# RMSNorm with ReLU on one core: from two DMA queues and strided 2 MB chunks to one queue in fixed order and contiguous 4 MB chunks

## The chip, the cores and the metric

The kernel runs on 1 core of one Trainium2 chip. The metric is the time of one execution on the device in microseconds (us); a lower number is better. In the views ACT is ScalarE, DVE is VectorE, POOL is GpSimd and SP is SyncE, which here only issues transfers; a DMA engine is one of the 16 that move the data. A profile describes one execution and gives its span, from the first to the last instruction; the measured time of the same execution is 1.8 to 2.1 us longer than its span.

A ratio is the mean time of one kernel's fast runs over the mean time of the other kernel's fast runs in the same rounds on the same chip, so it is not quite the ratio of the medians that are quoted beside it.

## The reference

```python
# x: [16, 1024, 512] float32 (32 MiB), gamma: [512] ones, eps = 1e-5
rms = np.sqrt(np.mean(x ** 2, axis=-1, keepdims=True) + eps)
x_norm = x / rms * gamma
return np.maximum(x_norm, 0).astype(np.float32)
```

There are 16,384 rows of 512 numbers. 33.55 MB have to be read and 33.55 MB written.

## The kernel before

Each of the 128 partitions owns 128 consecutive rows and takes them 8 at a time (16 KB per partition, 2 MB per transfer, neighbouring partitions 256 KB apart in DRAM). Loads are issued from SP (a hardware queue), stores from POOL (the software queue). The store converts a bf16 tile to f32 on its way. Gamma is spread over all partitions by a broadcast load of 256 KB that stands in front of the first load of x.

```python
xv = x2.rearrange("(p r) d -> p r d", p=P)
ov = out2.rearrange("(p r) d -> p r d", p=P)
K = 8
...
gamma_bcast = bass.AP(tensor=gamma.tensor, offset=gamma.offset,
                      ap=[[0, P], gamma.ap[0]])
nc.sync.dma_start(out=gamma_sbuf, in_=gamma_bcast)
...
for i in range(nchunks):
    s = i * K
    x_tile = pool.tile([P, K, d], F32)            # pool has 4 buffers
    nc.sync.dma_start(out=x_tile, in_=xv[:, s:s + K, :])
    ...
    nc.vector.tensor_mul(out=xg, in0=x_tile, in1=gammaK)
    for j in range(K):
        nc.scalar.activation(out=sq_scratch, in_=x_tile[:, j, :], func=Square,
                             accum_out=ss[:, j:j + 1])
    nc.scalar.activation(out=rms, in_=ss, func=Sqrt, bias=eps_sbuf, scale=inv_d)
    nc.vector.reciprocal(out=rstd, in_=rms)
    for j in range(K):
        nc.vector.tensor_scalar(out=o_tile[:, j, :], in0=xg[:, j, :],
            scalar1=rstd[:, j:j + 1], scalar2=0.0, op0=mult, op1=max)
    nc.gpsimd.dma_start(out=ov[:, s:s + K, :], in_=o_tile)
```

Of the kernel before, what the change touches and what calls it, by code (L numbers as in the profile page):

```python
# [1 line left out]

# [4 lines left out]


@with_exitstack
def kernel(  # L10
    ctx: ExitStack,
    tc: tile.TileContext,
    x: bass.AP,
    gamma: bass.AP,
    eps: bass.AP,
    out: bass.AP,
):
    nc = tc.nc
    P = nc.NUM_PARTITIONS

    x2 = x.flatten_outer_dims()
    out2 = out.flatten_outer_dims()
    n, d = x2.shape
    assert n % P == 0
    rows_per_part = n // P
    inv_d = 1.0 / d

    xv = x2.rearrange("(p r) d -> p r d", p=P)
    ov = out2.rearrange("(p r) d -> p r d", p=P)

    K = 8
    nchunks = rows_per_part // K
    assert rows_per_part % K == 0

    BF = mybir.dt.bfloat16
    F32 = mybir.dt.float32

    singles = ctx.enter_context(tc.tile_pool(name="singles", bufs=1))
    pool = ctx.enter_context(tc.tile_pool(name="pool", bufs=4))
    small = ctx.enter_context(tc.tile_pool(name="small", bufs=4))  # L40

    gamma_sbuf = singles.tile([P, d], F32)
    gamma_bcast = bass.AP(
        tensor=gamma.tensor,
        offset=gamma.offset,
        ap=[[0, P], gamma.ap[0]],
    )
    nc.sync.dma_start(out=gamma_sbuf, in_=gamma_bcast)  # L48

    eps_sbuf = singles.tile([P, 1], F32)  # L50
    nc.vector.memset(eps_sbuf, eps)  # L51

    sq_scratch = singles.tile([P, d], F32)

    gammaK = bass.AP(tensor=gamma_sbuf.tensor, offset=gamma_sbuf[:].offset,
                     ap=[gamma_sbuf[:].ap[0], [0, K], gamma_sbuf[:].ap[1]])

    for i in range(nchunks):
        s = i * K

        x_tile = pool.tile([P, K, d], F32)
        nc.sync.dma_start(out=x_tile, in_=xv[:, s:s + K, :])

        rstd = small.tile([P, K], F32)
        rms = small.tile([P, K], F32)
        ss = small.tile([P, K], F32)
        xg = pool.tile([P, K, d], F32)
        o_tile = pool.tile([P, K, d], BF)

        nc.vector.tensor_mul(out=xg, in0=x_tile, in1=gammaK)  # L70

        for j in range(K):
            ssj = ss[:, j:j + 1]
            nc.scalar.activation(out=sq_scratch, in_=x_tile[:, j, :],  # L74
                                 func=mybir.ActivationFunctionType.Square,
                                 accum_out=ssj)
        nc.scalar.activation(out=rms, in_=ss,  # L77
                             func=mybir.ActivationFunctionType.Sqrt,
                             bias=eps_sbuf, scale=inv_d)
        nc.vector.reciprocal(out=rstd, in_=rms)  # L80

        for j in range(K):
            rj = rstd[:, j:j + 1]
            nc.vector.tensor_scalar(  # L84
                out=o_tile[:, j, :], in0=xg[:, j, :],
                scalar1=rj, scalar2=0.0,
                op0=mybir.AluOpType.mult, op1=mybir.AluOpType.max,
            )

        nc.gpsimd.dma_start(out=ov[:, s:s + K, :], in_=o_tile)  # L90


# [1 line left out]
_INS = ['x', 'gamma', 'eps']  # L94
_OUTS = [((16, 1024, 512), 'float32')]
#: Inputs that are plain numbers.
_NUMBERS = {'eps': 9.999999747378752e-06}


# [26 lines left out]
```

## Time and profile before

| | before |
|---|---|
| time, median (range) | 165.87 us (165.78 to 166.01) |
| span of the profile | 164.0 us |
| DMA | 67.4 MB, 411 GB/s over the span |
| DVE busy, ACT busy | 75%, 61% |

These lines are from the page of the kernel before. The digits cut the span into 40 slices and give the busy share in tenths; the GB/s line has one number per slice; a queue's line gives its packets, megabytes and share of the time of 16 engines.

```profile
span 164.0 us, 565 instructions
...
DVE 122.8 (75%) x161; ACT 99.4 (61%) x274; POOL 8.9 (5%) x20
...
DMA  5999999999999999999999999999999999998994
GB/s 87 401 420 444 440 412 432 434 432 412 436 436 412 440 434 424 424 432 436 412 436 436 414 432 436 412 440 432 428 424 432 432 416 436 440 432 348 416 420 192
...
q1 hardware_dynamic: 2448, 33.82, 57.4%
q0 software_dynamic: 2304, 33.56, 49.4%
q14 instruction: 3, 0.02, 0.0%
```

The DMA engines are the busy ones and no compute engine is near 100%. The weak slices are the first (87 GB/s), one near the end (348) and the last.

The windows view of the kernel before gives, for each stretch: its length, busy time of DVE, ACT and POOL, the clock, the DMA share and GB/s.

```profile
core 0: us, DVE busy (x) ACT busy (x) POOL busy (x), PEclk, DMA share, GB/s
0.00:4.00 4.00, 0.06 (x1) 1.28 (x1) 0.20 (x4) 1.00 0.56 88
144.00:148.00 4.00, 4.00 (x3) 3.84 (x11) 0.00 (x0) 1.00 1.05 426
148.00:152.00 4.00, 3.96 (x11) 1.41 (x5) 0.53 (x1) 1.00 0.80 324
152.00:156.00 4.00, 2.15 (x6) 0.00 (x0) 0.53 (x1) 1.00 1.11 455
```

In the first 4 us little moves. From 148 to 152 us the DMA engines lose a quarter of their rate.

### The profile page before, as it was taken

The numbers are of one execution on the slowest core, as the hardware profiler recorded it, in microseconds if no ns is written. First come the engines' busy times: TensorE is split into PE (matmuls) and PEld (weight loads), VectorE is DVE, ScalarE is ACT, GpSimd is POOL, SyncE is SP. The second block draws the span as 40 slices with busy tenths as digits, with TensorE's granted clock in tenths as the row PEclk, the third lists the DMA queues.
The fourth block names the chain that finished last, engine by engine and source line by source line (L and its number), as shares of the span: only waits on it lengthen the run. The fifth ranks groups of instructions, "written<-read, shape, count | busy, mean of one in ns | idle before, by whom it ended". The sixth has DMA issues, their size and how long they took to land.

```text
span 164.0 us, 565 instructions
## 1 busy us (share of the span) xinstructions
DVE 122.8 (75%) x161; ACT 99.4 (61%) x274; POOL 8.9 (5%) x20
## 2 busy tenths in 40 slices
DVE  0029979999999999969498694968949498099600
ACT  3039999999993937739195682928649194094000
POOL 0000010011010101010100001010010101001100
DMA  5999999999999999999999999999999999998994
GB/s 87 401 420 444 440 412 432 434 432 412 436 436 412 440 434 424 424 432 436 412 436 436 414 432 436 412 440 432 428 424 432 432 416 436 440 432 348 416 420 192
DMA packets 4755, 67.40 MB, mean 411 GB/s; under 512 B 528, under 2 KB 528, under 8 KB 656
## 3 DMA queue, kind: packets, MB, share of 16 engines
q1 hardware_dynamic: 2448, 33.82, 57.4%
q0 software_dynamic: 2304, 33.56, 49.4%
q14 instruction: 3, 0.02, 0.0%
HBM read 33.82 MB, written 33.55 MB: 411 GB/s over the span
## 4 chain that ended last, share of the span: by engine, by line
issue 49%; DVE 27%; ACT 8%; DMA 6%; POOL 3%; POOLq 0%; SPq 0%
DVE xg L70 15%; DVE o_tile L84 11%; ACT sq_scratch L74 7%; DMA x_tile<-in_x_dram 6%; POOL out_dram L90 3%; ACT L77 1%; DVE rstd L80 1%; ACT rms L77 0%; POOLq L121 0%; SPq L48 0%; POOLq L90 0%
## 5 line engine op out<-in xcount | busy, mean ns | idle before, releaser
L74 ACT ACTIVATE sq_scratch<-x_tile 128x512 f32<-128x512 f32 x128 | 80.6, 630 | 48.8 <-DMA x_tile<-in_x_dram 45.3
L70 DVE TENSOR_TENSOR xg<-x_tile,gamma_sbuf 128x4096 f32<-128x4096 f32 x16 | 70.5, 4406 | 29.3 <-DMA x_tile<-in_x_dram 29.3
L84 DVE TENSOR_SCALAR o_tile<-xg,rstd 128x512 bf16<-128x512 f32 x128 | 52.1, 480 | 0.1
L74 ACT ACTIVATION_READ_ACCUMULATOR sq_scratch<-x_tile 128x1 f32 x128 | 23.9, 187 | 0.0
L90 POOL DMA_DIRECT2D out_dram<-o_tile x16 | 8.7, 541 | 145.9 <-DVE rstd L80 119.4
L77 ACT ACTIVATE rms<-ss,eps_sbuf 128x8 f32<-128x8 f32 x16 | 4.8, 301 | 0.5
L80 DVE RECIPROCAL rstd<-rms 128x8 f32<-128x8 f32 x16 | 3.1, 196 | 1.2 <-ACT rms L77 1.2
L74 ACT ACT_TABLE_LOAD x1 | 1.3, 1283 | 0.7 <-PEq L107 0.7
L77 ACT ACT_TABLE_LOAD x1 | 1.3, 1283 | 0.0
L51 DVE MEMSET eps_sbuf<- 128x1 f32 x1 | 0.1, 59 | 0.8 <-PEq L107 0.8
L107 POOL MEMSET const-float32-0.0<- 128x1 f32 x1 | 0.1, 99 | 0.2 <-issue 0.2
L107 POOL MEMSET const-bfloat16-1.0<- 128x1 bf16 x1 | 0.1, 102 | 0.0
L107 POOL MEMSET const-float32-1.0<- 128x1 f32 x1 | 0.1, 99 | 0.0
L107 POOL MEMSET const-uint8-127<- 128x1 uint8 x1 | 0.1, 99 | 0.0
## 6 DMA issues: line engine op xcount, KB each, us to landing
x_tile<-in_x_dram SPq DMA_DIRECT2D x16, 2048.0 KB, 26.4
out_dram<-o_tile POOLq DMA_DIRECT2D x16, 2048.0 KB, 21.3
gamma_sbuf<-in_gamma_dram SPq DMA_DIRECT2D x1, 256.0 KB, 5.4
```

What stands on the lines that cost most here:

```text
L51: nc.vector.memset(eps_sbuf, eps)
L70: nc.vector.tensor_mul(out=xg, in0=x_tile, in1=gammaK)
L74: nc.scalar.activation(out=sq_scratch, in_=x_tile[:, j, :], func=mybir.ActivationFunctionType.Square, accum_out=ssj)
L77: nc.scalar.activation(out=rms, in_=ss, func=mybir.ActivationFunctionType.Sqrt, bias=eps_sbuf, scale=inv_d)
L80: nc.vector.reciprocal(out=rstd, in_=rms)
L84: nc.vector.tensor_scalar(out=o_tile[:, j, :], in0=xg[:, j, :], scalar1=rj, scalar2=0.0, op0=mybir.AluOpType.mult, op1=mybir.AluOpType.max,)
L90: nc.gpsimd.dma_start(out=ov[:, s:s + K, :], in_=o_tile)
L107: nc = _bacc.Bacc("TRN2", target_bir_lowering=False, num_devices=1)
```

## The change

The intent is one stream of transfers that never pauses: all loads and stores in one hardware queue (SP) in an order fixed in the program, each transfer 4 MB and contiguous in DRAM (32 KB per partition), six slots of 4 MB that are loaded, computed in place in f32 and stored. Gamma becomes four loads of one 2 KB row on the ACT queue and a shuffle on DVE, and no longer stands in front of x. The squares that ACT throws away go to PSUM. The diff, cut to its core:

```diff
-    xv = x2.rearrange("(p r) d -> p r d", p=P)
-    ov = out2.rearrange("(p r) d -> p r d", p=P)
-    K = 8
+    xv = x2.rearrange("(c p k) d -> c p k d", p=P, k=16)
+    ov = out2.rearrange("(c p k) d -> c p k d", p=P, k=16)
+    K = 16
+    G = 8
+    nslots = 6
 ...
-    nc.sync.dma_start(out=gamma_sbuf, in_=gamma_bcast)
+    for q in range(0, P, 32):
+        nc.scalar.dma_start(out=gseed[q:q + 1, :], in_=gamma[None, :])
 ...
+    def load(i):
+        nc.sync.dma_start(out=slot[i % nslots], in_=xv[i])
+    def store(i):
+        nc.sync.dma_start(out=ov[i], in_=slot[i % nslots])
+    def compute(i):
+        xt = slot[i % nslots]
+        for g in range(ngroups):                  # two groups of 8 rows
+            a, b = g * G, (g + 1) * G
+            for j in range(a, b):
+                nc.scalar.activation(out=junk, in_=xt[:, j, :], func=ACTF.Square,
+                                     accum_out=ss[i][:, j:j + 1])
+            nc.scalar.activation(out=rms[i][:, a:b], in_=ss[i][:, a:b],
+                                 func=ACTF.Sqrt, bias=eps_sb, scale=inv_d)
+            nc.vector.tensor_mul(out=xt[:, a:b, :], in0=xt[:, a:b, :], in1=gammaG())
+            nc.vector.reciprocal(out=rstd[i][:, a:b], in_=rms[i][:, a:b])
+            for j in range(a, b):
+                nc.vector.tensor_scalar(out=xt[:, j, :], in0=xt[:, j, :],
+                    scalar1=rstd[i][:, j:j + 1], scalar2=0.0, op0=ALU.mult, op1=ALU.max)
 ...
-        nc.gpsimd.dma_start(out=ov[:, s:s + K, :], in_=o_tile)
+    for i in range(min(nslots, nchunks)):
+        load(i)
+    nc.vector.stream_shuffle(gamma_sb, gseed, [0] * 32)
+    for i in range(min(nslots, nchunks)):
+        compute(i)
+    nxt = nslots
     for i in range(nchunks):
+        store(i)
+        if i >= 1 and nxt < nchunks:
+            load(nxt)
+            compute(nxt)
+            nxt += 1
```

The order in the queue is load 0 to 5, store 0, store 1, load 6, store 2, load 7, store 3 to 7.

## The prediction

> **What bounds it now: DMA.** The page gives 67.4 MB in a 164.0 us span, 411 GB/s, the DMA engines at 9 tenths in 37 of 40 slices; DVE is 75% busy, ACT 61%. The landings in the trace sharpen this. Before the first store, 2 MB loads land every 4.90 us (428 GB/s); once a 2 MB load and a 2 MB store alternate, a pair takes 9.79 us (428 GB/s again). So one queue loading and two queues mixing run at one rate: 612 ns per 16 KB packet and engine. The Trainium skill, "DMA: Bandwidth & Descriptors", section "Specifications", gives a 435 GB/s fabric ceiling; this trace sits 2% below it. At 428, 67.1 MB need 156.7 us (estimate). Only about 7 us of the span are not that.
>
> **Where those 7 us are (packets of the trace).** The first packet starts at 1.75 us, but belongs to the gamma broadcast: 128 packets of 2 KB, many of 200 to 800 ns, so the first x packets start at 3.2 to 5.7 us, engine by engine. Near 148 to 152 us the queue runs thin (324 GB/s in the windows view; stores wait for DVE): about 1 us. The last store packet ends at 162.15, lands at 162.5; the span ends 1.5 us later.
>
> **What the change does.**
> - Gamma's broadcast becomes four 2 KB rows on the ACT queue plus a shuffle. x packets should start near 1.8 us: 1.5 to 3 us gained, all on the critical path. Largest term.
> - The dip near 150 us goes, as the last loads are queued early and stores follow back to back: about 1 us.
> - One queue instead of two, 4 MB contiguous chunks, 32 KB per partition: no change of rate, since 428 holds in both phases now; at most 1 us if packets grow beyond 16 KB.
> - Compute stays hidden. DVE per 8 rows: 4.29 + 3.17 + 0.11 = 7.57 us (chain of waits), 15.1 per chunk, 121 in all; now f32 to f32 in place, and I expect that to cost the same. New wait: the multiply overwrites x, so it waits for ACT's eight squares (8 x 0.755 = 6.0 us), exposed in the first group only. The first chunk lands near 12 us, DVE starts at 18 and ends near 140; the queue reaches the last store near 149 (1.8 + 15 x 9.8). Slack 9 us. The first store is ready at 34 us, the six loads occupy the queue until 60, and each reload waits for a store that finishes with another transfer queued. No bubble.
>
> **Sum.** 1.9 start + 156.7 data + 0.3 gamma remnants and skew + 0.4 landing + 1.5 end = 160.8, minus 0.5 for larger packets = 160.3 us span. The measured time is 1.9 us above the span now (165.87 against 163.97), so about 162.0 us: 2.3% faster, close to the 2% line. Range 159.9 to 164.2. Faster 0.63, same 0.32, slower 0.05.
>
> **What would show it.** Right: first x packets near 1.8 us; GB/s near 428 in every slice but the first and last; 9.8 us between 4 MB landings; last store issued before its turn. Wrong: DVE ending after 149 us; gaps in the GB/s line at load-to-store turns; first chunk landing after 13 us.
>
> **What would make it wrong.** In-place f32 scaling at half rate (0.6 us a row adds 25 us to DVE and makes it the bound, about 172 us); hardware-queue stores slower than the software-queue ones, never seen in this trace; a contiguous layout changing the 612 ns packet either way.

## The result, and the profile after

| | before | after |
|---|---|---|
| time, median (range), 4 runs each | 165.82 us (165.5 to 166.01) | 164.24 us (163.98 to 164.49) |
| ratio, 95% interval | 1 | 0.9904 (0.9888 to 0.9921) |
| span of the profile | 164.0 us | 162.0 us |

The kernel is 1% faster, which counts as the same at the 2% line. The prediction said 2.3% and 159.9 to 164.2 us; the measured time lies just outside the range. A later repeat of the changed kernel (run e14) gave 164.26 us and a ratio of 0.9914.

The same lines of the page, of the changed kernel:

```profile
span 162.0 us, 554 instructions
...
DVE 124.6 (77%) x164; ACT 98.5 (61%) x274; POOL 0.2 (0%) x4
...
DMA  6999899999999999998999999999999999999990
GB/s 227 421 405 502 388 413 493 390 421 477 396 421 471 396 388 388 461 445 388 463 437 404 453 445 404 453 437 396 461 429 445 429 421 445 429 421 445 437 413 16
...
q1 hardware_dynamic: 2304, 67.11, 96.9%
q14 instruction: 3, 0.02, 0.0%
q10 hardware_dynamic: 8, 0.01, 0.0%
```

The start is better (227 GB/s instead of 87). The ups and downs of the GB/s line are packets of 32 KB falling into one slice or the next. The end is odd: one slice at 413, then one at 16. The windows view of the changed kernel shows it closer:

```profile
0.00:4.00 4.00, 0.49 (x2) 0.79 (x1) 0.20 (x4) 1.00 0.69 229
144.00:148.00 4.00, 0.00 (x0) 0.00 (x0) 0.00 (x0) 1.00 0.99 426
148.00:152.00 4.00, 0.00 (x0) 0.00 (x0) 0.00 (x0) 1.00 0.97 418
152.00:156.00 4.00, 0.00 (x0) 0.00 (x0) 0.00 (x0) 1.00 1.02 442
156.00:160.00 4.00, 0.00 (x0) 0.00 (x0) 0.00 (x0) 1.00 0.51 221
160.00:162.00 2.00, 0.00 (x0) 0.00 (x0) 0.00 (x0) 1.00 0.00 0
```

The dip at 148 us is gone as predicted, and DVE is done before. But the half of the DMA time that is used from 156 to 160 us is nearly all before 158 us (410 GB/s from 156 to 158 us, 33 from 158 to 160 us), while the last landing comes only at 160.97 us, with nothing left to issue. The waits of SP, the engine that issues the transfers, in the changed kernel (who waited for what: total us, times, longest us) show that it was done early:

```profile
SPq L62 <- DVE slot L81: 94.5, 7, 20.7
SPq L59 <- DMA out_dram<-slot: 30.5, 2, 22.1
SPq L133 <- DMA out_dram<-slot: 17.6, 1, 17.6
```

The last line is SP at the end of the program, waiting 17.6 us for stores that it has long issued. So neither compute nor issue holds up the end; the DMA engines do. What they do can be read from the landings: each of the 16 engines reports separately when its sixteenth of a transfer has landed. The Trainium skill says so in "DMA: Bandwidth & Descriptors", section "Why a DMA increments its semaphore by 16 and not by 1" (the engines "finish independently"), and the traces here show the 16 separate times. This table is worked out from those times, for the last transfer of each profile. "Lag" is the last engine minus the ninth of 16.

```
profile                    9th engine   15th    last    lag   fetches in the run
before                        162.29   162.36  162.52   0.23   3
after                         158.86   159.42  160.97   2.11   3
e1  no gamma loads            158.98   160.99  161.22   2.24   3
e2  copy only                 158.67   158.86  159.03   0.35   0
e3  more instructions         158.85   160.82  162.44   3.59   9
e4  before + gamma rows       159.98   160.29  160.52   0.54   3
e5  copy + instructions       158.82   159.47  164.00   5.18   6
e6  strided rows              159.90   161.87  161.87   1.98   3
e7  16 KB runs                159.24   160.62  162.04   2.80   3
e8  two hardware queues       177.03   177.10  177.13   0.09   3
e9  markers                   158.86   161.36  161.40   2.54   3
e10 copy, alternating         159.09   159.22  159.65   0.56   0
e11 stores on POOL queue      158.69   159.14  160.20   1.50   3
e12 few instructions          158.94   159.70  160.26   1.31   0
e13 few, no gamma loads       158.74   159.13  159.99   1.26   0
e14 changed kernel again      158.81   160.54  161.27   2.46   3
```

In the changed kernel a middle engine has everything landed at 158.9 us, one engine needs until 161.0, and the program ends with that one. The lag does not come at once. From the same landings of the changed kernel it is 0.50 us at the landing of load 2 (32 us), 0.78 at load 4 (52 us), 1.05 at load 5 (63 us), 1.58 at load 6 (93 us), 1.34 at store 2 (102 us), 2.10 at load 7 (113 us) and 2.11 at the end. The instruction fetches of this profile (8 KB packets of queue 14) start at 31.5, 50.9 and 79.8 us.

### The profile page after: what moved, and what is told of

The parts are those of the page before. It is cut to its first block, busy times and chain, and to the rows that moved or that the text cites. A ratio compares the mean times of both kernels' runs of the same rounds, so it can differ in the third digit from the quotient of the medians.

```text
span 162.0 us, 554 instructions
## 1 busy us (share of the span) xinstructions
DVE 124.6 (77%) x164; ACT 98.5 (61%) x274; POOL 0.2 (0%) x4
## 4 chain that ended last, share of the span: by engine, by line
DVE 74%; DMA 8%; ACT 3%; issue 2%; DVEq 0%
DVE slot L78 43%; DVE slot L81 30%; DMA slot<-in_x_dram 8%; ACT junk L74 3%; DVE rstd L79 1%; DVEq L133 0%
## 5 line engine op out<-in xcount | busy, mean ns | idle before, releaser
L74 ACT ACTIVATE junk<-slot 128x512 f32<-128x512 f32 x128 | 76.8, 600 | 23.0 <-DMA slot<-in_x_dram 19.5
L78 DVE TENSOR_TENSOR slot<-slot,gamma_sb 128x4096 f32<-128x4096 f32 x16 | 70.7, 4418 | 4.2 <-ACT junk L74 4.2
L81 DVE TENSOR_SCALAR slot<-slot,rstd 128x512 f32<-128x512 f32 x128 | 52.1, 481 | 0.6
L74 ACT ACTIVATION_READ_ACCUMULATOR junk<-slot 128x1 f32 x128 | 23.8, 186 | 0.0
L76 ACT ACTIVATE rms<-ss,eps_sb 128x8 f32<-128x8 f32 x16 | 4.8, 301 | 0.5
L86 DVE MEMSET gseed<- 128x512 f32 x1 | 0.5, 485 | 0.9 <-PEq L119 0.9
L93 DVE STREAM_SHUFFLE gamma_sb<-gseed 128x512 f32<-128x512 f32 x1 | 0.7, 721 | 0.0
```

The lines of the kernel that those rows point to most:

```text
L74: nc.scalar.activation(out=junk, in_=xt[:, j, :], func=ACTF.Square, accum_out=ss[i][:, j:j + 1])
L76: nc.scalar.activation(out=rms[i][:, a:b], in_=ss[i][:, a:b], func=ACTF.Sqrt, bias=eps_sb, scale=inv_d)
L78: nc.vector.tensor_mul(out=xt[:, a:b, :], in0=xt[:, a:b, :], in1=gammaG())
L81: nc.vector.tensor_scalar(out=xt[:, j, :], in0=xt[:, j, :], scalar1=rstd[i][:, j:j + 1], scalar2=0.0, op0=ALU.mult, op1=ALU.max)
L86: nc.vector.memset(gseed, 0.0)
L93: nc.vector.stream_shuffle(gamma_sb, gseed, [0] * 32)
```

## The experiments

The theory at this point: a transfer is cut into 16 fixed shares, so the program ends with the slowest DMA engine, and some engines carry small extra transfers (fetches, gamma rows). The rivals: the late engine is late for a reason in the data transfers themselves, or in the traffic of ACT and DVE to the tiles, or compute is on the path after all.

| run | time, median (range) us | ratio to before (95%) | result |
|---|---|---|---|
| e1 no gamma loads | 164.07 (163.82 to 164.35) | 0.9895 (0.9878 to 0.9911) | right |
| e2 copy only | 161.67 (161.52 to 161.79) | 0.9751 (0.9737 to 0.9764) | wrong |
| e3 more instructions | 165.66 (165.48 to 165.87) | 0.9992 (0.9980 to 1.0005) | right |
| e4 before + gamma rows | 163.68 (163.62 to 163.76) | 0.9872 (0.9859 to 0.9886) | right |
| e5 copy + instructions | 166.08 (165.74 to 166.62) | 1.0024 (1.0007 to 1.0041) | wrong |
| e6 strided rows | 165.14 (164.72 to 165.56) | 0.9965 (0.9948 to 0.9981) | right |
| e7 16 KB runs | 164.28 (163.55 to 165.03) | 0.9912 (0.9886 to 0.9938) | right |
| e8 two hardware queues | 180.11 (179.78 to 182.42) | 1.0885 (1.0843 to 1.0926) | right |
| e9 markers | 164.28 (2 runs) | 0.9912 (0.9890 to 0.9933) | right |
| e10 copy, alternating | 163.63 (162.25 to 164.63) | 0.9870 (0.9832 to 0.9907) | wrong |
| e11 stores on POOL queue | 162.98 (162.66 to 163.98) | 0.9840 (0.9815 to 0.9864) | right |
| e12 few instructions | 162.85 (162.36 to 163.21) | 0.9818 (0.9802 to 0.9834) | wrong |
| e13 few, no gamma loads | 162.33 (161.92 to 162.93) | 0.9796 (0.9778 to 0.9814) | wrong |
| e14 changed kernel again | 164.26 (163.95 to 164.90) | 0.9914 (0.9897 to 0.9931) | right |

Most of these differences are under the 2% line (only e2 counts as faster, e8 as slower, e13 is unclear), so below they are read from the ratios to the kernel before, whose runs stood in the same rounds, and from the landings. The landings of a run are those of its one profile.

### e1: without the gamma loads

```diff
-    nc.vector.memset(gseed, 0.0)
+    nc.vector.memset(gseed, 1.0)
-    for q in range(0, P, 32):
-        nc.scalar.dma_start(out=gseed[q:q + 1, :], in_=gamma[None, :])
```

> The changed kernel with the four gamma loads taken out (gamma set to ones by a memset; it is ones in this input, so the result stays right). Theory S (one DMA engine ends 1.6 to 2.1 us after the others because it alone carries small extra transfers: four gamma rows of about 84 ns each and instruction fetches of about 0.32 us each): the spread of the last landing (last against middle engine, now 2.1 us) shrinks by about 0.35 us and the time by about 0.3 us, to about 163.9. Rival P (the late engine is late for a reason in the data transfers themselves): no change of the spread, under 0.1 us in time.

The ratio moved by 0.1% (0.9895 against 0.9904), within noise, and the lag stayed (2.24 us). So the gamma rows are not what makes the last engine late. In this profile two engines are late, at 160.99 and 161.22 us. This part of my theory fell.

### e2: copy only

```diff
     def compute(i):
-        (all of the computing)
+        pass
```

The gamma loads and the shuffle were taken out as well; the output is wrong.

> Wrong on purpose: the changed kernel's sixteen transfers in their order, with all computing and gamma taken out, so almost no instructions are fetched. Theory S: the last engine's lag at the end falls from 2.1 us to under 0.5 us; the start at 1.75 us, the long first packets (0.65 us) and the long packets at the first load-to-store turn (about 0.65 us near 58 us) stay; span about 160.0, time about 162.1. Rival P: the lag of about 2 us stays and the time is 163.5 or more. If the compute engines were on the path (rival C), the time would fall by over 3 us, to below 161.

161.67 us, 2.5% faster than before, and the lag is 0.35 us. The middle engine is hardly earlier than in the changed kernel (158.67 against 158.86): the gain lies in the late engine. Compute is not on the path. The queue lines of its page show what else left with the compute: there is no line for instruction fetches.

```profile
DMA packets 2304, 67.11 MB, mean 420 GB/s; under 512 B 256, under 2 KB 256, under 8 KB 256
...
q1 hardware_dynamic: 2304, 67.11, 98.1%
```

### e3: more instructions

```diff
+    pad = singles.tile([P, 1], F32, name="pad")
+    for _ in range(768):
+        nc.gpsimd.memset(pad, 0.0)
```

> The changed kernel with 768 tiny memsets (128x1, about 0.1 us each) on the idle POOL engine, which touch nothing else. Theory S: they need about six more 8 KB instruction fetches (64 bytes an instruction is an estimate from 8 KB fetches and the counts), each 0.32 us on some DMA engine; if they share the late engine, its lag grows by about 1 to 2 us and the time with it, to 165.2 to 166.2. Rivals P and C: within 0.2 us of the changed kernel.

The ratio went from 0.9904 to 0.9992 (about 1.5 us), the fetches from 3 to 9 and the lag to 3.59 us, with the middle engine unmoved at 158.85. POOL work that touches none of the kernel's data made it slower, as the theory said. e3 still had all the compute in it, so e5 asks the same of a kernel with none.

### e4: the kernel before, with only gamma changed

```diff
-    nc.sync.dma_start(out=gamma_sbuf, in_=gamma_bcast)
+    gseed = singles.tile([P, d], F32)
+    nc.vector.memset(gseed, 0.0)
+    for q in range(0, P, 32):
+        nc.scalar.dma_start(out=gseed[q:q + 1, :], in_=gamma[None, :])
+    nc.vector.stream_shuffle(gamma_sbuf, gseed, [0] * 32)
```

> The kernel before, with only its gamma broadcast replaced by the four row loads and the shuffle. My prediction's largest term says: x packets start near 1.8 us, not 3.2 to 5.7, and the time falls by 1.5 to 3 us, to 163 to 164.4. If the early start is given back later (to the wait of stores for DVE near 140 to 152 us, or to the late engine), less than 1 us is left.

163.68 us: 2.1 us gained, in the middle of what I expected, from this part alone. The windows view of e4, same columns as before:

```profile
0.00:4.00 4.00, 0.49 (x2) 1.13 (x1) 0.20 (x4) 1.00 0.61 209
144.00:148.00 4.00, 4.00 (x9) 3.05 (x9) 0.00 (x0) 1.00 1.07 434
```

209 GB/s in the first 4 us instead of 88. So this line of the change is worth more than the whole change (ratio 0.9872 against 0.9904 and 0.9914), and all the rest of it, the one queue, the order, the 4 MB chunks, costs 0.3% to 0.4% on balance. The landings say where: against e4 the middle engine of the changed kernel is done 1.1 us earlier (158.86 against 159.98), the last one 0.45 us later (160.97 against 160.52).

### e5: copy only, with instructions on POOL

```diff
     (e2, and)
+    pad = singles.tile([P, 1], F32, name="pad")
+    for _ in range(768):
+        nc.gpsimd.memset(pad, 0.0)
```

> Wrong on purpose: the copy-only kernel (161.67 us; all 16 engines end within 0.4 us of the middle one) with the 768 tiny memsets on POOL added, nothing else. Theory F (instruction fetches of 8 KB delay the DMA engine that carries them, each by 0.3 us and more): about six fetches appear in the trace at 10 to 145 us and some engines end late; if they share few engines as in the run with more instructions, the time rises by 0.6 to 1.6 us, to 162.3 to 163.3. Rival T (the late engines come from the traffic of ACT and DVE to the tiles, which copy-only also took out): no late engine, 161.7 again.

The direction was right and the size was far off: 166.08 us, 4.4 us more than e2, not 0.6 to 1.6. The trace of e5 has six fetches, at 11.0, 31.0, 52.3, 72.0, 92.0 and 112.3 us. Up to the first one POOL had started 74 instructions, then 202, 338, 464, 592, 721: one fetch about every 128 instructions. One single engine is late, at 164.00 us, with the other 15 done by 159.47; at every landing since the second fetch, too, only one is late. The page of e5:

```profile
GB/s 246 390 455 437 406 469 398 463 421 406 485 382 471 413 382 382 445 439 398 493 382 437 447 406 477 398 429 455 406 469 398 453 429 421 461 398 461 429 143 16
...
q1 hardware_dynamic: 2304, 67.11, 95.3%
q14 instruction: 6, 0.05, 0.1%
```

0.05 MB of fetches, 0.1% of the DMA time, and the kernel is 2.7% slower than e2, because all six went through one engine (read from the landings; the packets carry no engine number). The last slice (16 GB/s) is that engine alone, and so is the end of the one before (143). The second fetch moved its lag from 0.54 to 1.19 us between two neighbouring landings, the third from 1.20 to 2.04: 0.65 and 0.84 us, though the fetch's own packet is recorded with 0.31 us. Part of the rest is in the trace: the data packet that follows each fetch is longer too, by 0.09 to 0.35 us. Not all of the 5.18 us belongs to fetches: from 2.04 to 3.13 us the lag grew between the landings at 53.6 and 65.0 us, with no fetch between them, where the first store follows the loads. The memsets came with the fetches and no run parts the two, but POOL ran them at an even pace, and the lag sits on one engine and grows in steps. There is no ACT and no DVE work in this run, so the rival that blamed their traffic falls as an explanation of this lag.

### e6: old row layout, all else changed

```diff
-    xv = x2.rearrange("(c p k) d -> c p k d", p=P, k=16)
+    xv = x2.rearrange("(p c k) d -> c p k d", p=P, k=16)     # and ov the same
```

> The changed kernel with the old row layout (each partition owns 128 consecutive rows, so a 4 MB chunk is 128 runs of 32 KB, 256 KB apart, not one contiguous block). If contiguity in DRAM does nothing, as I predicted: within 0.3 us of the changed kernel (164.1). If it is what makes the steady packet short (1213 ns for 32 KB), packets get longer by 1% or more and the time rises by 1.5 us or more.

Neither. The median packet stayed at 1213 ns, so contiguity does nothing for the steady rate. Yet the time is 165.14 us, ratio 0.9965, 0.5% to 0.6% worse than the changed kernel. The middle engine ends 1.0 us later (159.90). The chains of packets in the trace show longer packets where the queue turns from loads to stores: near 58 to 60 us the engines lose 0.9 to 1.4 us on two packets (0.3 to 1.2 in the changed kernel), and near 90 us most lose another 0.4 to 0.8 us (0 to 0.3 in the changed kernel, but for its late engine). So contiguous chunks are worth about 0.9 us here, at the turns. Why, no run shows.

### e7: runs of 16 KB inside the 4 MB transfers

```diff
-    xv = x2.rearrange("(c p k) d -> c p k d", p=P, k=16)
+    xv = x2.rearrange("(c h p k) d -> c p h k d", h=2, p=P, k=8)   # ov and the tile side alike
```

> The changed kernel, same 4 MB transfers and order, but each partition's 32 KB come as two runs of 16 KB from the two halves of the chunk, so packets are 16 KB. If the packet size gave the 1% (1213 ns for 32 KB against 2 x 611.5): steady spacing of landings 9.78 instead of 9.68 us, time up by about 1.3 us, to 165.4, less what a smaller first packet saves (about 0.3). If the packet size does nothing: 164.1.

The packets became 16 KB (median 611 ns). Loads landed every 9.79 us instead of 9.72 and stores every 9.70 instead of 9.68. The middle engine ended 0.4 us later. The time (164.28 us, and a wide spread) shows no difference, so the packet size is worth less than the 1.3 us I gave it; the verdict on the time is open.

### e8: loads from ACT, stores from SP

```diff
-        nc.sync.dma_start(out=slot[i % nslots], in_=xv[i])
+        nc.scalar.dma_start(out=slot[i % nslots], in_=xv[i])     # and gamma's rows from SP
```

> The changed kernel with loads issued from ACT and stores from SP (and gamma's four rows from SP), so that stores may share the engines with loads from 34 us on. If the long packets near 58 us (0.6 to 0.7 us on every engine) are the price of all engines turning from loads to stores at once in one queue, they go, and the time falls by 0.4 to 0.8 us, to about 163.4; the late engines stay. If the one-queue order costs nothing: within 0.2 us of 164.1, or slower if mixed packets of 32 KB are less regular.

180.11 us, and it does not answer the question. ACT also computes the squares and works in program order, so the last reloads stood behind the squares of the chunks before: in the timeline of e8 the issue of load 6 comes only at 97.1 us.

```profile
97.13 0.33 ACTq L59 DMA_DIRECT2D slot<-in_x_dram  x1
```

The next two lines, from the page of e8, show the queues running dry.

```profile
DMA  6989989989999999999999999999938999200595
GB/s 235 472 369 456 463 375 456 458 368 375 449 441 406 449 441 412 441 456 406 427 463 405 427 463 412 419 471 412 412 103 375 405 419 471 118 0 0 235 471 235
```

### e9: markers

```diff
+    sets = {1: (3, 6, 9, 12, 15), 4: (1, 4, 7, 10, 13), 5: (2, 5, 8, 11, 14)}
     for i in range(min(nslots, nchunks)):
         load(i)
+        for k in sets.get(i, ()):
+            mk = singles.tile([16, 64], F32, name=f"mk{k}")
+            nc.sync.dma_start(out=mk[0:k, :], in_=x2[0:k, 0:64])
```

> A kernel for looking, not for its time: the changed kernel without the gamma loads, with 15 small marker loads of k rows (k = 1 to 15, 256 bytes each) between the big loads of the one queue. If a load of k rows goes to the k lowest-numbered engines, the number of markers in a chain of packets tells which engine it is. Theory F expects the same two late engines at the end as in the run without gamma loads (1.7 to 2.1 us behind the middle), each carrying a fetch near 32 and 80 us or near 51 us; the markers say which numbers they have. No claim about the numbers.

Again two late engines (161.36 and 161.40 us, the other 14 by 159.25), and the fetches at 33.3, 51.2 and 80.5 us. The Trainium skill, "DMA: Bandwidth & Descriptors", section "Why a DMA increments its semaphore by 16 and not by 1", says that a DMA from a hardware queue that runs on k engines takes the k lowest-numbered. The trace shows k landings of data for a marker of k rows. Read together, the landings name the late ones. Of the two landings of the marker with 2 rows one is late (63.98 against 62.38 us); the marker with 1 row was not late (52.01 us); among the 4 landings of the marker with 4 rows two are late (52.87 and 52.91 against 52.07 us). That makes them engine 1 and engine 2 or 3, and not engine 0, where the single gamma rows would go. This fits e1, in which taking the gamma rows away changed nothing. It rests on the skill's rule, which no run here tests by itself.

### e10: copy only, alternating

```diff
     (e2, and the order of the queue)
+    load(0)
+    for i in range(nchunks):
+        if i + 1 < nchunks:
+            load(i + 1)
+        store(i)
```

> Wrong on purpose: copy only, with loads and stores alternating from the start (load 0, load 1, store 0, load 2, store 1, ...), so about fifteen turns between reading and writing instead of six. If each turn costs what the first one did (0.5 to 0.7 us on every engine), the time rises from 161.7 by 3 us or more. If only the first store pays, or a turn costs 0.1 us: 161.4 to 162.5, and the long packets stand at the first store, near 22 us.

The times scatter from 162.25 to 164.63 us, so they don't decide. The one profile (of the fastest run) shows one packet of nearly every engine longer by 0.6 to 1.0 us at 20.8 to 21.0 us, when the first store follows, and almost nothing longer than 0.15 us at the turns after it. In that profile the first store costs once, wherever it stands (58 to 60 us in the changed kernel), and further turns cost little.

### e11: stores from POOL, all else changed

```diff
-        nc.sync.dma_start(out=ov[i], in_=slot[i % nslots])
+        nc.gpsimd.dma_start(out=ov[i], in_=slot[i % nslots])
```

> The changed kernel with its stores issued from POOL (the software queue, as before the change), loads still from SP, all else the same: two queues again, 32 KB per partition. If one queue in fixed order is worth something: slower than 164.1 by over 0.5 us. If the first turn of a single queue is what costs: the long packets near 58 us go and the time falls by about 0.5 us, the late engines staying.

162.98 us, ratio 0.9840, the fastest correct kernel: 1.6% faster than before and 0.7% faster than the changed kernel. So one queue for both is no gain here. Why e11 is faster is not isolated: the edit also changes the kind of queue (software for hardware) and the order (the first store has landed at 46.7 us in e11, and after 71 us in the changed kernel). The lag is 1.50 us, and the landings of e11 show it in steps: 0.66 us after the first fetch (load 2), 0.62 at the landing at 58 us, 1.32 at 85 us, after the fetch at 81.7 us, and 1.50 to 1.51 from 98 us to the end. In the changed kernel the step from 1.34 to 2.10 us at load 7 (113 us) came on top, 30 us after the last fetch of its trace.

### e12 and e13: the same traffic in few instructions

```diff
-            for j in range(a, b):
-                nc.scalar.activation(out=junk, in_=xt[:, j, :], func=ACTF.Square, accum_out=...)
+            nc.scalar.activation(out=junk, in_=xt[:, g * G:(g + 1) * G, :],   # 8 rows, one sum
+                                 func=ACTF.Square, accum_out=ss[i][:, g:g + 1])
 ...
-            for j in range(a, b):
-                nc.vector.tensor_scalar(out=xt[:, j, :], ..., scalar1=rstd[i][:, j:j + 1], ...)
+        nc.vector.tensor_scalar(out=xt, in0=xt, scalar1=rstd[i][:, 0:1], ...)  # 16 rows
```

The results are wrong (several rows share a scale). e13 also leaves out the gamma loads, as e1 did.

> Wrong on purpose: the changed kernel with the same loads, stores, queue order, waits and the same elements read and written by ACT and DVE, but in few instructions (squares 8 rows at a time with one sum; gamma multiply and scaling 16 rows at a time with one scale), so that ACT and DVE run about 50 and 30 instructions instead of about 300 and 180. Theory F: no instruction fetch falls into the run, the last landing is within 0.5 us of the middle one, and the time falls to that of copy-only, 161.5 to 162.2. Rival T (the late engines come from the traffic of ACT and DVE): the late engines stay, 163.5 to 164.3.

> Wrong on purpose: the run with few instructions, with the four gamma loads taken out as well. Theory F in its corrected form (the run ends with its latest DMA engine, so taking away one kind of small extra transfer shows only once the others are gone): in the run with few instructions the engine with the gamma rows was the last, 1.3 us behind the middle; without them no engine is over 0.5 us behind, and the time falls by 0.8 to 1.2 us to that of copy-only, 161.6 to 162.0, although the same removal gained nothing (0.1 us) while the fetches were there. If the gamma rows were not the cause of that last engine, the time stays at 162.8.

e12: no fetch in the run, 162.85 us, ratio 0.9818. That is 0.9% or about 1.4 us faster than the changed kernel, with the same elements through ACT and DVE; the page of e12 has 161 instructions instead of 554 and no instruction queue:

```profile
span 161.3 us, 161 instructions
...
q1 hardware_dynamic: 2304, 67.11, 97.4%
q10 hardware_dynamic: 8, 0.01, 0.0%
```

But it did not reach copy-only: a lag of 1.31 us was left, and the time lies between the forecasts of the two theories (161.5 to 162.2 and 163.5 to 164.3). Now the last engine is one whose chain of packets has gaps of 0.08 us at the four times of the gamma rows. e13 took those out: 162.33 us, 0.2% less than e12 with overlapping intervals, and the lag of its profile was still 1.26 us. So the expectation of e13 was missed: the gamma rows are not the cause of the rest. In both runs the lag is about 0.4 us at 101 us and jumps to 1.2 to 1.3 us at the landing of load 7 (111 us), where the queue turns from its last load to stores. The engine that was the last to arrive there loses most: 0.73 us on one packet in e12, and in e13 a gap of 0.43 us and 0.22 us on the next packet. In copy-only the engines arrive more evenly and the lag goes from 0.16 to 0.35 us only. What e13 has and copy-only has not is the work of ACT and DVE. Whether their traffic makes this rest is not tested: rival T is refuted for the part that left with the fetches, not for the 1.3 us that stayed.

### e14: the changed kernel again

> The changed kernel unaltered, as the yardstick of the same chip and rounds: 164.0 to 164.4, ratio to before 0.990; an engine about 2 us behind the middle one at the last landing.

As expected: 164.26 us, ratio 0.9914, two late engines (160.54 and 161.27 us).

## Why the prediction was wrong

The sum, term by term, for the span (from the trace; "data" is 128 packets of 1213 ns per engine; the third row is what remains for a middle engine, whose last packet ended at 158.5 us):

| term | predicted | measured |
|---|---|---|
| start to first packet of x | 1.9 | 2.0 (mean of 16 engines) |
| data | 156.2 | 155.3 |
| long packets at the start and at the first store | 0 | 1.2 |
| gamma remnants and skew | 0.3 | 2.1 |
| landing | 0.4 | 0.3 |
| end | 1.5 | 1.1 |
| span | 160.3 | 162.0 |

- **Bound by DMA, compute hidden: right.** DVE ended at 143 us (about 140 predicted), and copy-only, with no compute at all, is only 1.5% faster. In-place f32 scaling cost 481 ns a row against 480 before.
- **Gamma, "Largest term", "1.5 to 3 us gained, all on the critical path": right.** e4 gives it alone: 2.1 us.
- **"The dip near 150 us goes ... about 1 us": this step failed.** The dip went, and it gained nothing for the engine that ends last. In the kernel before, the landings around the dip show an engine that was 1.84 us behind the first at the store that landed at 147.96 us, and only 0.33 us at the one that landed at 157.67. In the dip (DMA share 0.80) the early engines ran dry and the late ones caught up. I had counted as a loss what was the slack of the early engines. Without it the lag stands at the end instead. The last engine did not pause: the last landings of the four stores around the dip, at 147.96, 152.81, 157.67 and 162.52 us, are 4.85 to 4.86 us apart, while the first landings of the second and third are 6.34 us apart. e8 shows the same by accident: where its queue runs dry, the lag falls from 1.64 us (load landed at 103 us) to 0.09. This reading rests on the landings; no run isolates the dip.
- **"0.3 gamma remnants and skew": the term that was mis-sized.** It measured 2.1 us. I treated 16 engines with fixed shares as one pipe with one rate. In part the lag comes from instruction fetches: e12, which has none, has 0.8 to 1.2 us less of it than the two profiles of the changed kernel (1.31 against 2.11 and 2.46) and is 1.4 us faster, and e3 and e5, which add fetches, add lag. The other part, 1.3 us, is there without any fetch (e12, e13); most of it appears where the queue turns from its last load to stores (seen in the landings of after, e12 and e13; not isolated by a run), and its cause stays open. It is not gamma's remnants (e1, e13).
- **"No bubble" at the turns: half right.** No gap came, but on most engines the packets around the first store were longer by 0.3 to 1.2 us in sum, and the first packet of most engines by 0.3 to 1.0 us (1.9 instead of 1.21 us). Both were absent from the sum.
- **Rate: better than I said.** 32 KB packets took 1213 ns, 432 GB/s over 16 engines, against 612 ns for 16 KB (428). The skill's ceiling of 435 GB/s, which the prediction cites, agrees with that: it is 0.7% away. "No change of rate" from the contiguous layout held for the steady packet, but e6 shows that the layout is worth about 0.9 us at the turns.
- **"428 holds in both phases", so one queue or two is the same: right for the rate, wrong for the end.** e11, with the stores in a second queue, ends 1.2 us earlier with packets of the same size; which of its differences does it is not isolated.

What stays open: why a late engine falls further behind at a turn and whether the traffic of ACT and DVE has a part in it, why the first store costs what it does, and why the packet after a fetch is longer.

## What to carry to other kernels

In a kernel bound by DMA, look at the 16 engines one by one: a transfer is cut into fixed shares, so the end is set by the engine that has fallen behind (2.1 us here), and the mean GB/s does not show it. A dip in the DMA rate is a loss only if the engines that end last were waiting in it, and here they were not. Before tuning queues and layouts, move small slow transfers out of the head of the stream, and count instructions too: in e5 a fetch came about every 128 of them, and six fetches cost 4.4 us, 0.7 us each on average, because one engine carried them all.

## What the Trainium skill lacked or had wrong

- "Runtime: NRT & Kernel Launch", section "Instruction fetch mechanics", calls the cost of a fetch "mostly hidden" and gives blocks of 16 KiB (256 instructions). Here the fetches were 8 KB packets, one about every 128 instructions of a stream, and in a kernel bound by DMA they were not hidden: six of them made the copy 4.4 us slower (161.67 to 166.08 us), 0.7 us each on average. The page speaks of the engine that runs the instructions; the cost here is that of the DMA engine that carries the fetch.
- "DMA: Bandwidth & Descriptors", section "Issuing engines are not separate DMA queues", says that issuing from several engines only saves the issue time. The steady rate agrees (428 GB/s with one queue or two), but moving the stores to POOL's queue took 1.2 us off the kernel (ratios 0.9840 and 0.9904 to 0.9914), and not through issue time, since SP waited 17.6 us at the end. The move also changed the order of loads and stores, so this doesn't show that the second queue by itself is what helped.
- "DMA: Bandwidth & Descriptors" tells of single engines that are usually slower, but no page has a lag that one engine builds up in steps over a run: 0.35 us at the last landing of sixteen transfers in e2 and 5.18 us with the same sixteen in e5.
- Pages give a fixed cost and a first-byte latency of a DMA, but none has the longer packets at the start and at the first store of a stream: 1.9 instead of 1.21 us for the first 32 KB packet of most engines, and 0.3 to 1.2 us per engine when the first store follows the loads.
